# A hand-ordered transformer trunk: attention output splits, output projection and last scan step reordered, seven weight splits moved to GpSimd

## The chip, the cores and the metric

One core of a Trainium2 chip runs the whole kernel. TensorE (PE) multiplies, VectorE (DVE) and ScalarE (ACT) work on its results, GpSimd (POOL) takes small side jobs, and SyncE (SP) issues the DMAs. The metric is the device time of one execution in microseconds. Before the change the median of three runs is 751.57 us (750.9 to 751.59).

## The reference

A trunk of two layers over 256 positions of width 1024: a sparse attention mixer (NSA), a gated MLP, a Mamba-2 mixer (SSD) and a second gated MLP, each between two RMS norms and added to the stream. Cut to what the change touches:

```python
def compress_tokens(t, pos, w1, w2):            # k_cmp and v_cmp, blocks of 32 with stride 16
    ...
    return jax.nn.gelu(flat @ w1) @ w2

def nsa_mixer(h, w_in, cmp_pos, cmp_w1, cmp_w2, w_out):
    proj = h @ w_in
    ...
    kc = compress_tokens(k_cmp, cmp_pos[0], cmp_w1[0], cmp_w2[0])
    vc = compress_tokens(v_cmp, cmp_pos[1], cmp_w1[1], cmp_w2[1])
    ...
    o = (gates[..., 0:1] * o_cmp + gates[..., 1:2] * o_sel + gates[..., 2:3] * o_win).astype(h.dtype)
    return o.reshape(b, s, NSA_Q_DIM) @ w_out

def ssd_scan(x, dt, a, bm, cm):                 # in chunks of 128
    ...
    w = cb[..., None] * lmat * dt_k[:, None]
    y = jnp.einsum("blsgh,bsghp->blghp", w, x_k)
    y = y + jnp.einsum("blgn,bghpn->blghp", c_k, state) * jnp.exp(acs)[..., None]
```

With 256 positions there are four selection blocks and all of them are selected, so the selected branch is a plain causal attention, as the window branch is.

## The kernel before

**Weights.** Every float32 matrix product is made of three rounded ones: a value is split into a high part (a cast on ACT, L56) and a low part (the difference, L57, on DVE or POOL), and high*high, high*low and low*high are added in PSUM. `Weights` (L71) loads a matrix in halves of 128x1024 from HBM into `raw` (512 KB each, L77), and splits each half into `whi` and `wlo`. `raw` has five buffers: the load of a half can be issued only when the half five places before it has been both cast and subtracted. `whi` and `wlo` have five buffers each too, which PE frees.

**Attention (to 160 us).** `ORDER` (L24) is a list of tokens, played by `token` (L458): v values, b the windows of compressed keys (b0) or values (b1), k keys, q queries, h one of four quarters of the compression matrix (h0 and h1 for keys, h2 and h3 for values), m the rest of the compression MLP (m0 keys, m1 values), p scores of a group's head, n softmax scaling, t a transposition of probabilities ("flip"), c and y the output of a group (into PSUM `po`), o the output projection. A `g` or `G` in a token puts the low part of its first or second half on POOL (`lows`, L460). Between bars the tokens are bound to the order of PE. The rest of the order, on every engine, is made by a scheduler from data dependences and the order of the code; within an engine instructions then run strictly in that order.

**The chain of m0** (L299 to L323) goes through all engines: `pc` (PSUM, the products of h0 and h1) is copied to `ph` by ACT, summed by PE (`pht`), copied to `xx` by ACT, worked on by DVE (`t`, L309 to L311), ACT (tanh, L312) and DVE (`hd`, L314, L315), and multiplied by PE (`pkc`, L319). Only then do the keys of compressed blocks exist, which the first scores read.

**Output.** `combine` (L443) adds a token's product to `po`, and with the last one splits `po` into `oT` at once (ACT and DVE). Token o (L489) multiplies two K tiles of `oT` with `nsa_out` into `acc`.

**The scan (460 to 500 us).** `SEQ` (L25) orders the Mamba scan likewise: x transposes a chunk of inputs into PSUM (`px`) and scales it on DVE (L712), m multiplies the masked decays (L732), y is the product of a group (`pys`, L736) and its addition on DVE (L748). `px`, `pys` and `pcb` share two PSUM buffers (tag t).

Of the kernel before, what the change touches and what calls it, by code (L numbers as in the profile page):

```python
# [20 lines left out]
EPS = 1e-6  # L21
T0, T1, N0, N1, SFILL, LAG = 5, 4, 2, 2, 2, 5
FA, FB, FN, CHAIN = 5, 8, 3, 0
ORDER = "v0 b0g k00w q00wG q01 k01 h0g u0 h1 m0 b1 h2 p00 p01 p02 p03 k10g q10 h3 n0 k11 q11 q20w p10 p11 m1 p12 q30w p13 n1 q21 t010 t000 t011w t001w q31 t012 p20 t013w | c0 y010 y011 y012 y013 y000 y001 | p21 t100 p22 t101w p23 t110 n2 t111w t112 p30 t113w | c1 y100 y101 y110 y111 y112 y113 | p31 t210 p32 t211w t200 p33 t212 t201w o00 t213w n3 | c2 y210 y211 y212 y213 y200 y201 | o01 t310 t300 t311w t301w t312 t313w | c3 y300 y301 y310 y311 y312 y313 o10 o11 |"  # L24
SEQ = "X00 X50 X01 X10 X11 X20 X60 X51 X21 X30 X31 X40 X70 X61 f0 X41 X71 Z00 E Z01 a0 Z10 f1 e00 e01 Z11 a1 e02 e03 x00 Z20 e10 e11 Z21 e12 e13 x10 m0 m1 x01 Z30 w0 Z31 y0 f2 w1 a2 e20 e21 e22 e23 x20 x11 Z40 f3 Z41 y1 m2 w2 x21 e30 e31 e32 | e33 a3 x30 | Z50 | m3 y2 x31 Z51 Z60 w3 | y3 | Z61 Z70 | Z71"  # L25
NEG = -1e30

C_ID, C_TRI, C_SUM, C_SEL, C_ONE, C_MS, C_N = 0, 128, 256, 316, 348, 476, 604
# [5 lines left out]
def trunk(ctx, tc, x, gains, consts, masks, params, nsa_in, nsa_vw, cmp_w1, nsa_out,  # L34
# [187 lines left out]
    def nsa(np_, xt, after):  # L222
# [220 lines left out]
        def combine(g, qt, n):  # L443
            po, ph = pos_[g, qt], phs[g, qt, n]
            b, kb = divmod(n, qt + 1)
            end = n == 2 * qt + 1
            for r in range(2):
                mm(po[64 * r:64 * r + 64], vs[:, kb, b, g, :], ph[:, r::2, :], start=False, stop=end)
            if end:
                qs = slice(128 * qt, 128 * qt + 128)  # L450
                split(oT[0][:, 2 * g:2 * g + 2, qs], oT[1][:, 2 * g:2 * g + 2, qs], po)

        oT = [one([128, KT, S], f"ot{n}", F32R) for n in range(2)]
        dummy = one([128, 1], "dummy")
# [3 lines left out]
        def token(z):  # L458
            kind, n, wide = z[0], [int(c) for c in z[1:] if c.isdigit()], "w" in z
            lows = [c for c in range(2) if "gG"[c] in z]  # L460
            if kind == "v":
                values()
            elif kind == "b":
                gs[n[0]] = blocks_of(n[0], wide, lows)
            elif kind == "k":
                keys(*n, wide, lows)
            elif kind == "h":
                kv, u = divmod(n[0], 2)
                if u == 0:
                    pc[kv] = pa([120, 256], "pc")  # L470
                hidden(pc[kv], kv, gs[kv], u, lows)
            elif kind == "u":
                setup()
                nc.sync.dma_start(mc16.rearrange("p a b -> p (a b)"), masks[:, :32])
            elif kind == "m":
                compressed(pc[n[0]], n[0])
            elif kind == "q":
                queries(*n, wide, lows)
            elif kind == "p":
                scores(*n)  # L480
            elif kind == "n":
# [510 lines left out]
```

## Time and profile before

| | before |
|---|---|
| median of 3 runs | 751.57 us |
| the profiled execution | 751.31 us |
| its span, first to last instruction | 749.5 us |
| PE busy | 720.9 us (96%) |
| DVE busy | 573.6 us (77%) |
| ACT busy | 465.5 us (62%) |
| POOL busy | 63.0 us (8%) |
| granted TensorE clock, mean | 0.991 |

PE is busy nearly all the time, so an edit counts where it makes or removes idle time of PE. Busy shares of the other engines are averages: near the end of the span and in the two MLPs they have room, in the attention stage DVE and ACT are at 80 and 68%.

### The profile page before, as it was taken

What the parts mean: (1) busy time and instruction counts of PE and PEld (TensorE: products, weight loads), DVE (VectorE), ACT (ScalarE), POOL (GpSimd) and SP (SyncE); (2) the same over time, 40 slices, a digit from 0 to 9 for tenths busy, and PEclk for the clock granted to TensorE, in tenths of its full rate; (3) what the DMA queues carried; (4) which work ended last, traced back from release to release, by engine and by line L of the source; (5) the groups of instructions that cost most, each with busy time, mean ns of one, the idle gap of its engine ahead of it and who ended that gap; (6) DMA issues with size and microseconds to landing.
All of it is one profiled execution on the core that took longest, in us unless ns stands there. A gap on an engine that the chain in (4) does not pass through costs nothing.

```text
span 749.5 us, 13757 instructions
## 1 busy us (share of the span) xinstructions
PE 720.9 (96%) x5300; PEld 665.4 (89%) x5300; DVE 573.6 (77%) x931; ACT 465.5 (62%) x881; POOL 63.0 (8%) x96
## 2 busy tenths in 40 slices
PE   7998999999999999999999999999989999999996
PEld 5998888679999999997899999898779999999995
DVE  4688998747977767777698878788888967776783
ACT  4576777646665556565785687766556656555651
POOL 2210111211000000000100000024120000000000
PEclk7999999999999999999999999999999999999999
DMA  8864421315656665666355565125645665666531
GB/s 313 276 219 156 161 89 56 112 57 169 218 177 197 195 189 179 188 211 199 118 170 164 189 210 160 67 85 176 215 144 163 204 192 173 199 192 194 176 112 57
DMA packets 35426, 125.95 MB, mean 168 GB/s; under 512 B 4064, under 2 KB 4384, under 8 KB 35360
## 3 DMA queue, kind: packets, MB, share of 16 engines
q1 hardware_dynamic: 35360, 125.07, 51.6%
q8 instruction: 42, 0.69, 0.4%
q14 instruction: 24, 0.20, 0.1%
HBM read 124.00 MB, written 1.05 MB: 167 GB/s over the span
## 4 chain that ended last, share of the span: by engine, by line
PE 74%; DVE 12%; ACT 7%; DMA 3%; issue 2%; POOL 1%; SPq 0%; DVEq 0%; POOLq 0%; ACTq 0%
PE pu L61 43%; PE acc L61 18%; PE pv L61 6%; DVE wlo L57 4%; ACT P L388 2%; PE pt L65 2%; ACT whi L56 1%; DVE P L412 1%; ACT junk L126 1%; PE po L61 1%; DMA gain<-in_gains 1%; PE py L61 1%; DMA raw<-in_ssd_in 1%; DMA raw<-in_ffn_down 1%; DMA raw<-in_ssd_out 1%
## 5 line engine op out<-in xcount | busy, mean ns | idle before, releaser
L57 DVE TENSOR_TENSOR wlo<-raw,whi 128x1024 fp32r<-128x1024 f32 (+1 forms) x220 | 268.1, 1225 | 81.8 <-ACT whi L56 81.2
L56 ACT CAST whi<-raw 128x1024 fp32r<-128x1024 f32 x223 | 231.1, 1044 | 108.6 <-PE pu L61 58.3
L61 PE MATMUL pu<-xhi,whi 128*128 128x256 f32 x1056 | 296.3, 281 | 0.1
L61 PE MATMUL pu<-xhi,wlo 128*128 128x256 f32 x1056 | 295.1, 280 | 0.0
L61 PE MATMUL pu<-xlo,whi 128*128 128x256 f32 x1056 | 294.7, 279 | 0.0
L61 PEld LDWEIGHTS pu<-xhi,whi 128*128 128x128 f32 x1056 | 198.5, 188 | 2.0 <-DVE kd L53 0.3
L61 PEld LDWEIGHTS pu<-xlo,whi 128*128 128x128 f32 x1056 | 198.6, 188 | 1.2
L61 PEld LDWEIGHTS pu<-xhi,wlo 128*128 128x128 f32 x1056 | 198.4, 188 | 0.1
L524 DVE SCALAR_TENSOR_TENSOR cc<-pu,pr,cc 128x255 f32<-128x255 f32 (+2 forms) x248 | 111.3, 478 | 6.4 <-ACT cc L518 3.3
L61 PE MATMUL acc<-whi,hm 128*128 128x512 f32 x352 | 114.6, 390 | 1.0 <-ACT hm L56 1.0
L61 PEld LDWEIGHTS acc<-whi,hm 128*128 128x128 f32 x352 | 66.1, 188 | 14.7 <-ACT hm L56 1.5
L61 PE MATMUL acc<-wlo,hm 128*128 128x512 f32 x176 | 68.9, 392 | 0.0
L518 ACT ACTIVATE cc<-pu,pr 128x256 f32<-128x256 f32 x112 | 57.7, 558 | 8.9 <-PE pu L61 8.8
L56 ACT CAST hm<-cc 128x256 fp32r<-128x256 f32 x44 | 17.8, 405 | 44.9 <-DVE cc L552 44.9
L117 POOL TENSOR_SCALAR ms<-ss 128x1 f32<-128x1 f32 x16 | 7.7, 479 | 420.0 <-ACT junk L126 420.0
L61 PE MATMUL acc<-whi,gw 128*128 128x512 f32 x128 | 41.3, 397 | 0.0
L61 PEld LDWEIGHTS acc<-wlo,hm 128*128 128x128 f32 x176 | 33.0, 188 | 5.6
L61 PE MATMUL pv<-whi,xhi 128*128 128x256 f32 (+1 forms) x128 | 36.8, 300 | 1.0 <-ACT whi L56 0.6
L61 PE MATMUL pv<-whi,xlo 128*128 128x256 f32 (+1 forms) x128 | 35.6, 296 | 1.0 <-DVE xlo L57 0.9
L61 PE MATMUL pv<-wlo,xhi 128*128 128x256 f32 (+1 forms) x128 | 36.0, 293 | 0.0
L57 DVE TENSOR_TENSOR hm<-cc,hm 128x256 fp32r<-128x256 f32 x44 | 18.6, 423 | 14.6 <-ACT hm L56 14.6
L61 PEld LDWEIGHTS acc<-whi,gw 128*128 128x128 f32 x128 | 24.0, 188 | 5.2
(212 smaller groups left out, 885.2 us busy)
## 6 DMA issues: line engine op xcount, KB each, us to landing
raw<-in_ffn_up SPq DMA_DIRECT2D x88, 512.0 KB, 4.4
raw<-in_ffn_down SPq DMA_DIRECT2D x44, 512.0 KB, 4.6
raw<-in_ssd_in SPq DMA_DIRECT2D x40, 512.0 KB, 4.7
raw<-in_nsa_in SPq DMA_DIRECT2D x18, 512.0 KB, 5.2
raw<-in_ssd_out SPq DMA_DIRECT2D x16, 512.0 KB, 4.5
gain<-in_gains SPq DMA_DIRECT2D x8, 512.0 KB, 5.0
raw<-in_cmp_w SPq DMA_DIRECT2D x8, 512.0 KB, 5.2
raw<-in_nsa_out SPq DMA_DIRECT2D x8, 512.0 KB, 4.1
```

The source lines that it names most:

```text
L56: r = copy(hi, src)
L57: eng.tensor_tensor(lo, src, hi.bitcast(F32), op=OP.subtract)
L61: last_mm[0] = nc.tensor.matmul(*a, **k)
L65: last_mm[0] = nc.tensor.transpose(*a)
L117: nc.gpsimd.tensor_scalar(ms, a, b, EPS, op0=OP.mult if isinstance(b, float) else OP.add, op1=OP.add)
L126: nc.scalar.activation(junk, src[c], AF.Square, scale=1.0 / 32, accum_out=ss[:, c:c + 1])
L388: nc.scalar.activation(P[qt][:, hh, b, :], sx[:, b, :], AF.Exp, bias=mx[:, qt, b:b + 1], accum_out=sums[:, qt, hh, b + 1:b + 2])
L412: eng.tensor_scalar(P[qt][:, hh, b, :], P[qt][:, hh, b, :], rr[:, qt, hh, b + 1:b + 2], 1.0, op0=OP.mult, op1=OP.mult)
L518: nc.scalar.activation(c, ps, AF.Identity, bias=pr[:, base + nt:base + nt + 1], scale=pr[:, base + nt - 1:base + nt])
L524: nc.vector.scalar_tensor_tensor(c[:, s:], ps[:, :S - s], wv, c[:, s:], op0=OP.mult, op1=OP.add)
```

## The change

1. The tokens h0g, h1, h2, h3 become h0gG, h1gG, h2gG, h3gG: the low parts of all eight halves of the compression matrix are made on POOL, where one of the eight was before.
2. `combine` no longer splits `po`. A new function `heads_out` and a token s do it; s0 and s1 stand behind the next group's first scores, s2 and s3 among the flips and outputs.
3. Token o takes one K tile instead of two (o00 becomes o000 and o001), and these are spread among the flips of the last two groups.
4. In SEQ, `y2 x31` becomes `x31 y2`.

```diff
-ORDER = "v0 b0g k00w q00wG q01 k01 h0g u0 h1 m0 b1 h2 p00 p01 p02 p03 k10g q10 h3 n0 k11 q11 q20w p10 p11 m1 p12 q30w p13 n1 q21 t010 t000 t011w t001w q31 t012 p20 t013w | c0 y010 y011 y012 y013 y000 y001 | p21 t100 p22 t101w p23 t110 n2 t111w t112 p30 t113w | c1 y100 y101 y110 y111 y112 y113 | p31 t210 p32 t211w t200 p33 t212 t201w o00 t213w n3 | c2 y210 y211 y212 y213 y200 y201 | o01 t310 t300 t311w t301w t312 t313w | c3 y300 y301 y310 y311 y312 y313 o10 o11 |"
+ORDER = "v0 b0g k00w q00wG q01 k01 h0gG u0 h1gG m0 b1 h2gG p00 p01 p02 p03 k10g q10 h3gG n0 k11 q11 q20w p10 p11 m1 p12 q30w p13 n1 q21 t010 t000 t011w t001w q31 t012 p20 t013w | c0 y010 y011 y012 y013 y000 y001 | p21 s0 t100 p22 t101w p23 t110 n2 t111w t112 p30 t113w | c1 y100 y101 y110 y111 y112 y113 | p31 s1 t210 p32 t211w t200 p33 t212 t201w o000 t213w n3 | o001 c2 y210 y211 y212 y213 y200 y201 o010 s2 t310 t300 o011 t311w t301w o100 t312 t313w o101 c3 y310 y311 y312 y313 y300 y301 s3 o110 o111 |"
@@ -446,9 +446,11 @@
             end = n == 2 * qt + 1
             for r in range(2):
                 mm(po[64 * r:64 * r + 64], vs[:, kb, b, g, :], ph[:, r::2, :], start=False, stop=end)
-            if end:
+
+        def heads_out(g):
+            for qt in (1, 0):
                 qs = slice(128 * qt, 128 * qt + 128)
-                split(oT[0][:, 2 * g:2 * g + 2, qs], oT[1][:, 2 * g:2 * g + 2, qs], po)
+                split(oT[0][:, 2 * g:2 * g + 2, qs], oT[1][:, 2 * g:2 * g + 2, qs], pos_[g, qt])
 
         oT = [one([128, KT, S], f"ot{n}", F32R) for n in range(2)]
         dummy = one([128, 1], "dummy")
@@ -486,13 +488,15 @@
                 compressed_out(*n)
             elif kind == "y":
                 combine(*n)
+            elif kind == "s":
+                heads_out(*n)
             else:
-                u, i = n
+                u, i, k = n
                 if not accs:
                     accs.extend([ps_([128, 512], "acc") for c in range(2)] for i in range(2))
                 if u not in wos:
                     wos[u] = weights(nsa_out[u], 2, D, lows=lows)
-                out_mm(accs[i], i, [(oT, 2 * u + k, wos[u], k) for k in range(2)], u == 0, False)
+                out_mm(accs[i], i, [(oT, 2 * u + k, wos[u], k)], u + k == 0, False)
 
         accs = []
         rigid = False
```

The scheduler's order follows from this. On POOL, in the attention stage (wlo_548 is the low part of the second half of h0, wlo_576 and wlo_582 those of h1, wlo_694 and wlo_700 of h2, wlo_899 and wlo_905 of h3; wlo_813 belongs to keys and was there before):

```order
 L57 TENSOR_TENSOR wlo_451<-raw_448,whi_450 128x1024
 L57 TENSOR_TENSOR wlo_542<-raw_539,whi_541 128x1024
+L57 TENSOR_TENSOR wlo_548<-raw_545,whi_547 128x1024
+L57 TENSOR_TENSOR wlo_576<-raw_573,whi_575 128x1024
+L57 TENSOR_TENSOR wlo_582<-raw_579,whi_581 128x1024
+L57 TENSOR_TENSOR wlo_694<-raw_691,whi_693 128x1024
+L57 TENSOR_TENSOR wlo_700<-raw_697,whi_699 128x1024
 L57 TENSOR_TENSOR wlo_813<-raw_810,whi_812 128x1024
+L57 TENSOR_TENSOR wlo_899<-raw_896,whi_898 128x1024
+L57 TENSOR_TENSOR wlo_905<-raw_902,whi_904 128x1024
```

Seven subtractions have come from DVE, six of them in one row with wlo_542 and wlo_813 around them.

On ACT, around the chain of m0, before (ph_601, xx_606 and t1_608 are m0's; whi_699 is the second half of h2, whi_812 and whi_818 the halves of the next keys):

```order
L301 COPY ph_601<-pc_538 120x256
L56 CAST whi_699<-raw_697 128x1024
L307 COPY xx_606<-pht_603 128x120
L56 CAST whi_812<-raw_810 128x1024
L312 ACTIVATE t1_608<-t1_608 128x120
L56 CAST whi_818<-raw_816 128x1024
L322 CAST kd0_136<-pkc_616 128x4x15
```

and after the change:

```order
L56 CAST whi_699<-raw_697 128x1024
L301 COPY ph_601<-pc_538 120x256
L56 CAST whi_812<-raw_810 128x1024
L307 COPY xx_606<-pht_603 128x120
L312 ACTIVATE t1_608<-t1_608 128x120
L322 CAST kd0_136<-pkc_616 128x4x15
L56 CAST whi_818<-raw_816 128x1024
```

The casts of raw_697 and raw_810 have moved ahead of the copies ph and xx, so that each copy now stands behind a load.

On PE, the flips of the last group, before (pt are the flips, acc the output projection):

```order
L61 MATMUL acc_1687<-whi_1696,ot1_208 128x512
L65 MATMUL pt_1781<-ident_74,cs1_200 128x128
L65 MATMUL pt_1785<-ident_74,P1_1522 128x128 x4
L65 MATMUL pt_1792<-ident_74,cs1_200 128x128
L65 MATMUL pt_1796<-ident_74,P0_1521 128x128 x4
L65 MATMUL pt_1803<-ident_74,P1_1522 128x128 x4
L65 MATMUL pt_1810<-ident_74,P0_1521 128x128 x4
L65 MATMUL pt_1817<-ident_74,P1_1522 128x128 x4
L65 MATMUL pt_1824<-ident_74,P1_1522 128x128 x4
```

and after:

```order
L65 MATMUL pt_1786<-ident_74,cs1_200 128x128
L65 MATMUL pt_1790<-ident_74,P0_1521 128x128 x4
L61 MATMUL acc_1686<-whi_1696,ot0_207 128x512
L61 MATMUL acc_1686<-wlo_1697,ot0_207 128x512
L61 MATMUL acc_1686<-whi_1696,ot1_208 128x512
L61 MATMUL acc_1687<-whi_1696,ot0_207 128x512
L61 MATMUL acc_1687<-wlo_1697,ot0_207 128x512
L61 MATMUL acc_1687<-whi_1696,ot1_208 128x512
L65 MATMUL pt_1803<-ident_74,P1_1522 128x128 x4
L65 MATMUL pt_1810<-ident_74,P0_1521 128x128 x4
```

The eight flips stood in one row; now six matmuls of the projection stand behind each pair.

## Rows read from the trace of the kernel before

**Rows 1.** Busy time by stretch, 40 to 160 us, the sum (PE, PEld, DVE, ACT, POOL):
```profile
sum 120.00, PE 111.53 PEld 98.76 DVE 96.87 ACT 82.17 POOL 17.76; mean PE 9.29 PEld 8.23 DVE 8.07 ACT 6.85 POOL 1.48
```
**Rows 2.** Waits of PE from 40 to 165 us: total us, times, longest.
```profile
PE pkc L61 <- DVE hd L315: 2.1, 1, 2.1
PE sb L61 <- ACT P L388: 1.6, 3, 0.8
PE sa L61 <- ACT P L388: 1.6, 3, 1.3
...
PE pt L65 <- ACT ct L424: 0.8, 1, 0.8
...
PE pt L65 <- ACT pht L435: 0.4, 2, 0.2
```
**Rows 3.** The chain that ended last, 42 to 64 us: start, us, what.
```profile
46.97 1.82 DVE wlo L57 x2
...
54.68 2.33 DVE t L310
...
57.04 0.30 DVE t L311
...
58.29 0.66 PE pkc L61 x4
```
**Rows 4.** Timeline of POOL, 25 to 60 us: start, us, what [idle before <- releaser].
```profile
54.55 2.38 POOL L57 TENSOR_TENSOR wlo<-raw,whi 128x1024 fp32r<-128x1024 f32 x1 [15.35 <-ACT whi L56]
```
**Rows 5.** Timeline of DVE, the same operation of m0 and of m1.
```profile
54.60 2.41 DVE L310 TENSOR_SCALAR t<-t 128x120 f32<-128x120 f32 x1
...
89.52 0.21 DVE L310 TENSOR_SCALAR t<-t 128x120 f32<-128x120 f32 x1
```
**Rows 6.** Timeline of ACT, 42 to 55 us, casts of weight halves.
```profile
42.78 2.00 ACT L56 CAST whi<-raw 128x1024 fp32r<-128x1024 f32 x2
...
45.30 2.01 ACT L56 CAST whi<-raw 128x1024 fp32r<-128x1024 f32 x2
...
53.42 1.06 ACT L56 CAST whi<-raw 128x1024 fp32r<-128x1024 f32 x1 [0.43 <-DMA raw<-in_nsa_in]
```
**Rows 7.** Timeline of the DMA queue (SP), 48 to 50 us.
```profile
48.22 1.46 SPq L77 DMA_DIRECT2D raw<-in_nsa_in  x2
```
**Rows 8.** The page, part 6: DMA issues, count, KB each, median us to landing.
```profile
raw<-in_nsa_out SPq DMA_DIRECT2D x8, 512.0 KB, 4.1
```
**Rows 9.** Timeline of POOL, 502 to 506 us.
```profile
502.62 1.29 POOL L792 TENSOR_TENSOR sq<-sq 128x512 f32<-128x512 f32 x1 [13.16 <-ACT sq L791]
503.99 1.61 POOL L793 TENSOR_TENSOR sq<-sq 128x256 f32<-128x256 f32 x1
```
**Rows 10.** Timeline of DVE, the same stretch.
```profile
503.46 1.54 DVE L57 TENSOR_TENSOR wlo<-raw,whi 128x1024 fp32r<-128x1024 f32 x1 [1.17 <-ACT whi L56]
```
**Rows 11.** Timeline of PE, 72 to 80 us, the quarter h3 of the compression.
```profile
76.48 0.38 PE L61 MATMUL pc<-whi,gs 128*120 128x256 f32 x1 [0.41 <-ACT whi L56]
...
77.74 0.38 PE L61 MATMUL pc<-wlo,gs 128*120 128x256 f32 x1
```
**Rows 12.** Timeline of DVE, the masked decays of the last scan step.
```profile
484.10 2.36 DVE L732 SCALAR_TENSOR_TENSOR E<-E,cb 128x1024 f32<-128x1024 f32 x2
```
**Rows 13.** Timeline of PE, the transposes of the last scan input.
```profile
487.39 0.63 PE L65 MATMUL pt<-ident,xs 128*128 128x128 f32 x4 [1.58 <-DVE xs L748]
```
**Rows 14.** The chain that ended last, the projection behind them, a later `pys`.
```profile
488.02 5.61 PE pu L61 x48
...
494.98 1.90 PE py L61 x32
```
**Rows 15.** Timeline of PE, the first transposes.
```profile
9.88 1.54 PE L65 MATMUL pt<-ident,xn 128*128 128x128 f32 x6 [3.34 <-DVE xn L146]
```
**Rows 16.** Busy time by stretch after them (PE, PEld, DVE, ACT, POOL, PEclk, DMA, GB/s).
```profile
10.00:16.00 6.00, 5.43 (x24) 4.90 (x25) 4.92 (x7) 4.70 (x9) 0.86 (x2) 0.50 1.02 411
16.00:20.00 4.00, 4.00 (x23) 4.00 (x23) 3.78 (x5) 1.91 (x4) 0.00 (x0) 0.60 1.01 386
```

More of the change, by code (lines that the diff above doesn't have):

```diff
@@ L23 @@
 FA, FB, FN, CHAIN = 5, 8, 3, 0
-ORDER = "v0 b0g k00w q00wG q01 k01 h0g u0 h1 m0 b1 h2 p00 p01 p02 p03 k10g q10 h3 n0 k11 q11 q20w p10 p11 m1 p12 q30w p13 n1 q21 t010 t000 t011w t001w q31 t012 p20 t013w | c0 y010 y011 y012 y013 y000 y001 | p21 t100 p22 t101w p23 t110 n2 t111w t112 p30 t113w | c1 y100 y101 y110 y111 y112 y113 | p31 t210 p32 t211w t200 p33 t212 t201w o00 t213w n3 | c2 y210 y211 y212 y213 y200 y201 | o01 t310 t300 t311w t301w t312 t313w | c3 y300 y301 y310 y311 y312 y313 o10 o11 |"
-SEQ = "X00 X50 X01 X10 X11 X20 X60 X51 X21 X30 X31 X40 X70 X61 f0 X41 X71 Z00 E Z01 a0 Z10 f1 e00 e01 Z11 a1 e02 e03 x00 Z20 e10 e11 Z21 e12 e13 x10 m0 m1 x01 Z30 w0 Z31 y0 f2 w1 a2 e20 e21 e22 e23 x20 x11 Z40 f3 Z41 y1 m2 w2 x21 e30 e31 e32 | e33 a3 x30 | Z50 | m3 y2 x31 Z51 Z60 w3 | y3 | Z61 Z70 | Z71"
+ORDER = "v0 b0g k00w q00wG q01 k01 h0gG u0 h1gG m0 b1 h2gG p00 p01 p02 p03 k10g q10 h3gG n0 k11 q11 q20w p10 p11 m1 p12 q30w p13 n1 q21 t010 t000 t011w t001w q31 t012 p20 t013w | c0 y010 y011 y012 y013 y000 y001 | p21 s0 t100 p22 t101w p23 t110 n2 t111w t112 p30 t113w | c1 y100 y101 y110 y111 y112 y113 | p31 s1 t210 p32 t211w t200 p33 t212 t201w o000 t213w n3 | o001 c2 y210 y211 y212 y213 y200 y201 o010 s2 t310 t300 o011 t311w t301w o100 t312 t313w o101 c3 y310 y311 y312 y313 y300 y301 s3 o110 o111 |"
+SEQ = "X00 X50 X01 X10 X11 X20 X60 X51 X21 X30 X31 X40 X70 X61 f0 X41 X71 Z00 E Z01 a0 Z10 f1 e00 e01 Z11 a1 e02 e03 x00 Z20 e10 e11 Z21 e12 e13 x10 m0 m1 x01 Z30 w0 Z31 y0 f2 w1 a2 e20 e21 e22 e23 x20 x11 Z40 f3 Z41 y1 m2 w2 x21 e30 e31 e32 | e33 a3 x30 | Z50 | m3 x31 y2 Z51 Z60 w3 | y3 | Z61 Z70 | Z71"
 NEG = -1e30
```

## The prediction

> **What bounds the kernel now.** I read the page first: PE is busy nearly all the span, so the question is where it idles. The sum of the stretches from 40 to 160 us shows 111.53 us of PE in 120 [rows 1]: about 8.5 us idle at most to be won in the attention stage, where nearly all of the change lies. Then the waits of PE [rows 2] say what ends the idle time: once 2.1 us for `hd` (the compression chain m0), 3.2 us in six places for the exponentials that free score buffers, and 1.2 us for the flips' copies. Then the chain of waits from 42 to 64 us [rows 3] shows why `hd` is late: the path runs through DVE's weight splits and through one operation, L310, of 2.33 us, before it comes to PE's `pkc` at 58.29. All times that follow are in the clock of this execution.
>
> **Seven splits on POOL, the key chain.** Removed from DVE: seven subtractions of about 1.1 us (the one at 503.46 took 1.54, of which it stood 0.45 behind a POOL operation that ended at 503.91) [rows 9, 10], some 8 us of 96.87 that DVE works there [rows 1]. Added to POOL: seven of 2.38 us [rows 4], twice as long. POOL has the time; what counts is who waits.
>
> Three things hang on the end of a split: PE's products of that half, the buffer `raw` of that half, and DVE, since the two engines block each other. For the last, L310 took 2.41 us beside a POOL split that ran from 54.55 to 56.93, and 0.21 us in the second chain with no POOL work beside it [rows 4, 5]: it waited until POOL had ended. And it goes both ways: POOL's L793 took 1.61 us when DVE's split was waiting before it [rows 9, 10]. I read this as taking turns.
>
> So, step by step. The cast of h0's second half ends at 43.8 (first of two from 42.78, 1.0 each) [rows 6]. POOL: h0's second half to 46.2, h1's first to 48.6. DVE's split for b1 is waiting by then (its cast ended at 47.31 [rows 6], and only one scaling of queries more stands before it), so it takes the next turn, to 49.7; h1's second half then runs to 52.1. Before, DVE had done it by 48.2 (the splits from 46.97) [rows 3]. PE comes to it at about 49.6 and idles 2.5 us; the products end at 53.1.
>
> The `raw` buffer of h1's second half is the one that the first half of the next keys needs. That load was issued at 48.22, right behind the split [rows 7], and its cast waited for the landing until 53.42, so 5.2 us [rows 6]. Now the issue is at 52.1, the landing at 57.3, the cast done at 58.4. On ACT the copy `xx` of m0 used to stand ahead of this cast and now stands behind it: it ends at about 58.6. With the cast done POOL starts that half's split at 58.4 (the two of h2 are over by 58.0) and holds DVE until 60.8; L309 and L310 come in the middle, as L310 did before. From L311 to `pkc` it takes 58.29 - 57.04 = 1.25 us [rows 3], with 0.2 for L310: `pkc` at 62.3 in place of 58.29, 4.0 later. Five more matmuls stand behind `pkc` than before, at 5.61/48 = 0.117 us [rows 14]: 0.6. The scores start **4.6 us late**.
>
> Bounds: with POOL keeping the port (h1 done at 51.0), the landing in 4.1 us as the loads of the output weights did [rows 8], and no blocked L310, `pkc` comes at 58.2 and the loss is 0.5 us; if both L309 and L310 are blocked by different POOL splits, 2.4 more than my value, 7.0. I take 4.6, because the collision with the split of the same keys is in the trace of before [rows 4, 5] and both orders of ACT put that cast next to `xx`.
>
> The Trainium skill speaks against the move: "SBUF — State Buffer", section "Who interferes with whom", has one port pair shared by the two engines as a lock that the first holds for its whole instruction while the other fully blocks, for a two-port mode of DVE and for a DVE instruction with two SBUF inputs. L310 agrees (2.41 us beside 0.21). By that rule DVE's split for b1, with two SBUF inputs, takes its turn as I count it; by the row alone only operations like L310 are blocked, h1 would be done 1.1 us earlier and the sum be that much smaller.
>
> **The last quarter, h3.** PE waited for the cast of its second half until 76.48 and found the low part ready at 77.74 [rows 11]. On POOL the low part is 2.38 us behind the cast: 78.85. PE now asks for it after eight matmuls, at 77.4, but its arrival is what the next products wait for: 78.85 - 77.74 = **1.1 us late**. The first half's low part costs less than the 0.41 that it waited for that cast anyhow [rows 11], so nothing. Bounds 0 (PE, 4.6 late, finds other work) and 2.4 (DVE takes a turn first).
>
> **Output splits behind the next scores.** Nothing is added or removed: the same casts and subtractions, later. ACT's exponentials come earlier by the 0.4 to 0.8 us of those casts, but only for the group after the first does ACT's order change. The waits for exponentials are 3.2 us [rows 2]; with DVE lighter by two splits after 62 us I take a quarter, **-0.8**, between 0.5 lost (DVE's remaining splits bunch in front of the maxima) and all 3.2 won.
>
> **Output projection among the flips.** The flips waited 0.8 and 0.4 us for copies of the ones before [rows 2]. Six matmuls now stand behind each pair of flips, over 1 us of PE work, which covers these waits. The projection's own inputs are long split, and its last part still stands behind the last outputs, as before. **-1.2**, between 0 and -1.4.
>
> **Scan.** PE waited 1.58 us at 487.39 for L748 to free a buffer [rows 13]. Now the transposes come first, but L712, which empties their buffer, stands behind both L732 on DVE (484.10 to 486.46 [rows 12]), so it ends at 487.1; the second half of the product `pys` needs that buffer, takes 0.95 (half of 1.90), and the projection follows at 488.1, where it was at 488.02 [rows 14]. The wait changes its name: **0**, within 0.8 lost (POOL's addition comes later beside DVE) and 1.6 won.
>
> **The sum.** 4.6 + 1.1 - 0.8 - 1.2 + 0 = 3.7 us on the profiled execution's 751.31, of which 749.5 are span: 755.0. That execution is 0.26 under the median, which I leave inside the range: **755.0 us**, slower by 0.5%. By its own bounds the likeliest case lies at 753.2 to 757.5.
>
> **The rivals.**
> *A. DVE was the bound and is freed: faster.* The chain before `pkc` is DVE's splits and L310 [rows 3]. If five fewer splits let m0 run early, the loss is the 0.5 of the lower bound, h3 costs nothing, and -1.8 of the 3.2, -1.4 at the flips are kept: -2.7, 748.6. It decides for this if `xx` ends before 56.5 and POOL isn't in the middle of a split then. Against it: five buffers of `raw`, and the row of L310.
> *B. The loss is absorbed: no change.* The head costs about 2.5 (landing in 4.1 us and one blocked operation only), half of the 3.2 is won back since PE is late and ACT has caught up: 2.5 + 0.5 - 1.6 - 1.2 = 0.2, 751.5. For it: six waits that can shrink. Against it: the exponentials wait for PE's scores, and shift with them.
> *C. The clock falls too: slower still.* PE idled 3.34 us before 9.88, and the granted clock then stood at 0.50 (the 1.2 GHz level) from 10 to 16 and averaged 0.60 to 20, at least 9 us at the low level [rows 15, 16]. In my count PE idles about 3.9 us before `pkc`. If that is enough, PE runs at half speed until about 70: half of some 8 us of work lost, 4.0, less 0.5 of waits that it hides: 758.5. For it: the idle time is longer than that one. Against it: it is split by short work, and the 2.1 us of before left the clock at 1.00.
>
> **Chances.** A 0.20, B 0.15, forecast 0.45, C 0.20. A measurement of this kernel can tell about 0.2%, 1.5 us. Slower: the forecast and C, 0.65; same 0.15; faster 0.20. The range from 749.4 to 758.8 leaves half of A below, and the upper part of C above.
>
> **What would show it.** Right: POOL with splits back to back from 43.8 to about 58, `pc` waiting over 1.5 us for a low part, `pkc` waiting for `hd` by 3 us or more, L309 or L310 over 2 us, waits for `ct` and `pht` gone, and a wait of over 1 us inside `pys` in the scan. Wrong: `pkc` before 60, the loads after h1 issued as early as before, or a gain in the flips beyond 1.4 us. A clock row below 1.00 between 58 and 75 us says C.

## The result, and the profile after

The changed kernel takes 759.84 us (median of 4, 758.79 to 761.59), the kernel before 751.24 us beside it: ratio 1.0121 [1.0106, 1.0136], 8.6 us slower where 3.7 were forecast. The profiled execution took 759.34 us; its span is 757.0, which is 7.5 more than before.

Where the 7.5 us lie is seen when the attention stage is cut at four events that both traces have: the first product of h0 (`pc`), the first score (`sb`), the first product into `pvc` (the end of m1), and the first transposition of the next stage. Busy time by stretch (length, then PE, PEld, DVE, ACT, POOL, granted clock, DMA share, GB/s), before:

```profile
46.17:60.01 13.84, 10.80 (x91) 10.40 (x89) 12.79 (x17) 9.17 (x16) 2.38 (x1) 1.00 0.88 293
60.01:92.68 32.67, 30.86 (x254) 29.78 (x252) 29.39 (x70) 25.30 (x74) 3.53 (x8) 1.00 0.43 138
92.68:167.70 75.02, 70.95 (x498) 58.33 (x498) 54.69 (x127) 47.51 (x147) 13.58 (x28) 1.00 0.25 83
```

and after:

```profile
46.02:64.50 18.48, 13.37 (x90) 12.74 (x89) 10.87 (x12) 9.41 (x16) 13.74 (x6) 0.86 0.65 229
64.50:101.28 36.78, 32.41 (x252) 30.78 (x251) 32.13 (x70) 26.79 (x76) 11.32 (x10) 0.98 0.45 146
101.28:175.18 73.90, 70.26 (x498) 58.30 (x498) 52.44 (x125) 45.97 (x145) 15.41 (x28) 1.00 0.23 71
```

I call the stretches I, II and III. I is 4.64 us longer, II 4.11 longer, III 1.12 shorter: 7.63, which is the whole difference. PE's busy time in I is longer only because its clock was lower (0.86 of 18.48 us: 2.6 us lost). In II 2.6 us are more waiting, and 1.5 us a longer busy time of PE for the same matmuls: group by group the counts are those of before. The clock is the smaller part of these 1.5, since in w_after (below), with 1.00 in II, PE is still busy for 32.02 us there; what makes the rest is not shown. III is shorter by 0.7 of busy time, again for the same matmuls, and by 0.4 of waits.

The waits of PE from 40 to 165 us, after (total us, times, longest), which answer to [rows 2]:

```profile
PE pc L61 <- POOL wlo L57: 4.0, 4, 2.1
PE pkc L61 <- DVE hd L315: 2.7, 1, 2.7
PE pvc L61 <- DVE hd L315: 1.4, 1, 1.4
PE pt L65 <- ACT ct L424: 1.2, 2, 0.8
PE sb L61 <- ACT P L388: 1.0, 1, 1.0
PE sb L61 <- DVE A L361: 0.6, 2, 0.5
PE sa L61 <- ACT P L388: 0.5, 2, 0.4
```

Two waits are new, `pc` for POOL's low parts and `pvc` for the end of m1; the exponentials' waits have halved (3.2 to 1.5), those for `ct` have grown. PE also waits 0.6 us for `A`, the scaled queries.

The head, step by step. POOL (answers to [rows 4]):

```profile
43.73 16.03 POOL L57 TENSOR_TENSOR wlo<-raw,whi 128x1024 fp32r<-128x1024 f32 x6 [4.70 <-ACT whi L56]
76.29 2.38 POOL L57 TENSOR_TENSOR wlo<-raw,whi 128x1024 fp32r<-128x1024 f32 x1 [16.53 <-ACT whi L56]
82.08 2.37 POOL L57 TENSOR_TENSOR wlo<-raw,whi 128x1024 fp32r<-128x1024 f32 x1 [3.41 <-ACT whi L56]
```

DVE beside it (answers to [rows 5]):

```profile
47.75 1.82 DVE L57 TENSOR_TENSOR wlo<-raw,whi 128x1024 fp32r<-128x1024 f32 x1 [0.24 <-ACT whi L56]
...
49.94 2.92 DVE L57 TENSOR_TENSOR wlo<-raw,whi 128x1024 fp32r<-128x1024 f32 x1
...
57.40 2.51 DVE L309 TENSOR_TENSOR t<-xx 128x120 f32<-128x120 f32 x1 [4.08 <-ACT xx L307]
59.94 0.22 DVE L310 TENSOR_SCALAR t<-t 128x120 f32<-128x120 f32 x1
```

Of the seven moved splits five stand in this row, and the sixth of the row is the keys' split, which was on POOL before; h3's two follow by themselves. The six have no gap, 16.03 us for what alone takes 6 times 2.38, or 14.3; the rest is DVE's turns. DVE's own two splits of b1 took 1.82 and 2.92 instead of some 1.2, and L309 stood until the keys' split ended at 59.76.

ACT and the DMA queue (answer to [rows 6, 7]):

```profile
56.16 1.05 ACT L56 CAST whi<-raw 128x1024 fp32r<-128x1024 f32 x1 [2.33 <-DMA raw<-in_nsa_in]
57.12 0.25 ACT L307 COPY xx<-pht 128x120 f32<-128x120 f32 x1
```

```profile
46.17 2.67 SPq L77 DMA_DIRECT2D raw<-in_cmp_w  x2
51.80 3.65 SPq L77 DMA_DIRECT2D raw<-in_nsa_in  x4
57.46 2.66 SPq L77 DMA_DIRECT2D raw<-in_cmp_w  x2
```

The keys' load goes out at 51.80 (48.22 before), and `xx` stands behind its cast. So `pkc` comes 15.43 us behind the first `pc` instead of 12.12.

Behind the first scores, PE waits for both low parts of h3 and at `pvc` (answers to [rows 11], where the low part was ready):

```profile
78.73 0.38 PE L61 MATMUL pc<-wlo,gs 128*120 128x256 f32 x1 [0.49 <-POOL wlo L57]
```

```profile
84.50 0.38 PE L61 MATMUL pc<-wlo,gs 128*120 128x256 f32 x1 [1.06 <-POOL wlo L57]
```

```profile
101.28 0.51 PE L61 MATMUL pvc<-pr,hd 128*15 128x64 f32 x6 [1.43 <-DVE hd L315]
```

The granted clock, stretch by stretch, around the two long waits:

```profile
50.00:52.00 2.00, 0.17 (x1) 0.17 (x2) 2.00 (x2) 1.78 (x3) 2.00 (x2) 1.00 0.55 207
52.00:54.00 2.00, 2.00 (x13) 2.00 (x14) 1.28 (x2) 1.42 (x2) 2.00 (x1) 0.65 0.52 131
54.00:56.00 2.00, 2.00 (x12) 2.00 (x11) 0.00 (x0) 0.00 (x0) 2.00 (x2) 0.50 0.91 320
56.00:62.00 6.00, 3.32 (x28) 3.12 (x28) 3.52 (x5) 1.51 (x3) 3.76 (x2) 1.00 0.87 329
62.00:64.00 2.00, 2.00 (x14) 2.00 (x14) 0.66 (x2) 1.26 (x2) 0.00 (x0) 0.71 0.44 147
64.00:66.00 2.00, 2.00 (x11) 2.00 (x10) 1.99 (x3) 1.05 (x1) 0.00 (x0) 0.50 0.07 18
```

It fell to 0.50 (the 1.2 GHz level) twice, from 52.6 to 56.0 and from 62.8 to 66.2, each time while PE was busy again after idling 2.1 and 2.7 us. Before, it stayed at 1.00 here.

The scan: the wait at the transposes [rows 13] is gone and stands inside `pys` instead, where L716 comes behind both L736 (L712 and L732 of the kernel before; answers to [rows 12]):

```profile
494.36 1.09 PE L61 MATMUL py<-E,xd 128*64 128x128 f32 x16 [1.74 <-DVE xd L716]
```

```profile
491.34 2.36 DVE L736 SCALAR_TENSOR_TENSOR E<-E,cb 128x1024 f32<-128x1024 f32 x2
493.62 0.68 DVE L716 TENSOR_TENSOR xd<-pt,dt 128x512 f32<-128x512 f32 x1
```

From the next stage's first transposition to the end it is 581.8 us in both.

### The profile page after: what moved, and what is told of

Read it like the earlier page. It is cut to its first block, busy times and chain, and to the rows that moved or that the text cites. A ratio compares the mean times of both kernels' runs of the same rounds, so it can differ in the third digit from the quotient of the medians.

```text
span 757.0 us, 13760 instructions
## 1 busy us (share of the span) xinstructions
PE 723.8 (96%) x5300; PEld 668.2 (88%) x5300; DVE 570.7 (75%) x924; ACT 465.3 (61%) x881; POOL 87.2 (12%) x103
## 4 chain that ended last, share of the span: by engine, by line
PE 70%; DVE 8%; ACT 5%; issue 3%; DMA 2%; POOL 1%; DVEq 0%; POOLq 0%; ACTq 0%
PE pu L61 41%; PE acc L61 18%; PE pv L61 4%; DVE wlo L57 3%; PE pt L65 2%; ACT whi L56 1%; ACT P L388 1%; PE po L61 1%; ACT junk L126 1%; PE py L61 1%; DVE P L412 1%; DMA raw<-in_ssd_in 1%; DMA raw<-in_ffn_down 1%; DMA raw<-in_ssd_out 1%; DVE gw L793 1%
## 5 line engine op out<-in xcount | busy, mean ns | idle before, releaser
L57 DVE TENSOR_TENSOR wlo<-raw,whi 128x1024 fp32r<-128x1024 f32 (+1 forms) x213 | 263.6, 1243 | 77.8 <-ACT whi L56 77.3
L61 PE MATMUL pv<-whi,xhi 128*128 128x256 f32 (+1 forms) x128 | 36.8, 300 | 1.0 <-ACT whi L56 0.6
L57 POOL TENSOR_TENSOR wlo<-raw,whi 128x1024 fp32r<-128x1024 f32 x11 | 28.0, 2562 | 40.4 <-ACT whi L56 40.4
L57 DVE TENSOR_TENSOR hm<-cc,hm 128x256 fp32r<-128x256 f32 x44 | 18.6, 423 | 14.6 <-ACT hm L56 14.6
```

Source lines behind the costliest of these rows:

```text
L57: eng.tensor_tensor(lo, src, hi.bitcast(F32), op=OP.subtract)
L61: last_mm[0] = nc.tensor.matmul(*a, **k)
```

## The experiments

Ratios are to the kernel before, run on the same chip.

**The two halves of the change.** Everything but the seven subtractions, and the subtractions alone:

```diff
 e1_no_pool (from the changed kernel)        e2_pool_only (from the kernel before)
-h0gG u0 h1gG m0 b1 h2gG ... h3gG            -h0g u0 h1 m0 b1 h2 ... h3
+h0g u0 h1 m0 b1 h2 ... h3                   +h0gG u0 h1gG m0 b1 h2gG ... h3gG
```

> The changed kernel with the four tokens h0g, h1, h2, h3 as before, so that DVE makes the seven low parts again; output splits, projection by single K tiles and the scan's swap stay. Theory (all of the loss is the seven subtractions on GpSimd): 750.3 to 751.2 us, 0 to 0.9 us under the kernel before (the traces show 0.5 us won at the flips and 0.16 lost in the scan); the wait of pkc is 2.1 us again and the granted clock stays at 1.00 from 50 to 70 us. Rival (the later output splits or the projection cost something themselves, hidden in the trace of after by the later scores): 752.5 or more.

> The kernel before with nothing but h0gG, h1gG, h2gG, h3gG: the seven subtractions alone. Theory (they are the whole loss): 8 to 9.5 us over the kernel before, some 760 us, with PE waiting some 2 us for a low part near 52 us and some 2.7 us for hd near 61 us, and the granted clock at 0.5 in two stretches of some 3.4 us. Rival (the other edits give part of the loss, or only the sum of both makes the waits long enough): 4 to 6 us over the kernel before.

e1: 749.99 us, 0.9982 [0.9971, 0.9992], faster by 1.35 us; I 13.38, II 32.69, III 73.68, with the clock at 1.00 in all three. Its III:

```profile
92.22:165.90 73.68, 70.22 (x499) 58.34 (x498) 54.73 (x127) 47.59 (x147) 14.50 (x28) 1.00 0.26 85
```

PE's busy time in III is that of the changed kernel (70.26), with II as before. So the 0.7 us of shorter busy time come from the other edits and not from a move of work between the stretches. e2: 760.68 us, 1.0127 [1.0111, 1.0142], with both waits and both falls. The seven subtractions are the whole loss; the other three edits gain a little, most of it (1.34 us in the profiles) in III.

**Is that gain the scan's?** e1 with `y2 x31` as before:

```diff
-m3 x31 y2 Z51
+m3 y2 x31 Z51
```

> The kernel before with the later output splits and the projection by single K tiles only: the scan's order and all of GpSimd's work as before. Theory (the scan's swap only renames a wait; what e1_no_pool gains, 1.35 us, is all in the attention stage): the time of e1_no_pool within 0.5 us, some 749.7. Rival 1 (in e1_no_pool's profile the granted clock fell for 3.4 us in the scan, and the swap causes that): 1 to 1.7 us under e1_no_pool. Rival 2 (the gain is the swap's): the time of the kernel before.

750.07 us, 0.9985 [0.9975, 0.9994]: the time of e1, so the swap gains nothing. The profiles show more than the times. From the second group of `py` products to the next stage's first `acc` it is 30.4 us without the swap (before, e2, e8) and 30.8 to 30.9 with it (the changed kernel twice, e10): the swap loses about 0.5 us, too little for the times. In e1's profile, where the clock is at 0.50 from 486.9 to 490.3, the same stretch takes 32.39 us; that execution took 750.89 us, 0.9 over its median. And in e8's profile the clock is at 0.50 from 58.2 to 61.6, behind PE's wait of 1.81 us at `pkc`: with the head's order as in e1 its I takes 14.40 us instead of 13.38, and II gives nothing back (32.72, 32.69).

**Which subtractions?** Keys only, values only, and h3 alone and alone left out:

```diff
 e5_h01  (from before)      -h0g u0 h1       +h0gG u0 h1gG
 e6_h23  (from before)      -h2 ... h3       +h2gG ... h3gG
 e17_h3  (from before)      -h3              +h3gG
 e18_no_h3 (from after)     -h3gG            +h3
```

> The kernel before with h0gG and h1gG only: three of the seven subtractions on GpSimd, those of the keys' compression; h2 and h3 stay on DVE. Theory (the head of the loss is these three: PE's wait for h1's second half, the load behind it, xx and L309 or L310 held by GpSimd; the rest of the loss is h2 and h3): PE waits about 2 us for h1's second low part, pkc comes 2.5 to 3.5 us later than in the kernel before, no wait of over 1 us for h3's low parts or for pvc, and 4 to 6 us over the kernel before with whatever clock falls follow. Rival 1 (it takes the whole row of six on GpSimd to hold the loads; three hold nothing): at most 1.5 us over the kernel before. Rival 2 (these three are all of the loss): 8 us or more.

> The kernel before with h2gG and h3gG only: the four subtractions of the values' compression on GpSimd. Theory: pkc as in the kernel before within 1 us, PE waits about 0.5 and 1.0 us for the low parts of h3 and some 1.4 us at pvc, 2 to 3.5 us over the kernel before, no fall of the clock near 50 to 66 us. Rival 1 (h2's splits on GpSimd alone hold the loads and pkc): pkc 2 us or more later, 5 us or more over the kernel before. Rival 2 (the waits for h3 and pvc come only from the late head): at most 1 us over the kernel before.

> The kernel before with h3gG only: the last two of the seven subtractions on GpSimd. Theory (the part of the loss behind the first scores, some 3 us, is these two: PE waits for both low parts, and the values' chain m1 ends in a wait at pvc): first scores as in the kernel before within 0.5 us, PE waits of some 0.5 to 0.8, 1.0 and 1.4 us at the two low parts and at pvc, no fall of the clock before pvc, and 2.5 to 4 us over the kernel before. Rival (these waits need the late head; on time, they are taken from waits that were there already): at most 1 us over the kernel before.

> The changed kernel with h3 for h3gG: its last two low parts on VectorE again, the others on GpSimd. Theory: the first scores as late as in the changed kernel, no wait at pvc or for h3's low parts, 2.5 to 4 us under the changed kernel, some 5 over the kernel before. Rival (the late head alone sets the loss, h3's waits replace others): within 1 us of the changed kernel.

| | us | ratio | I | II | III |
|---|---|---|---|---|---|
| before | | | 13.84 | 32.67 | 75.02 |
| e5 (h0, h1) | 754.62 | 1.0042 [1.0029, 1.0054] | 17.67 | 33.42 | 75.11 |
| e6 (h2, h3) | 758.25 | 1.0104 [1.0087, 1.0120] | 18.57 | 36.81 | 74.79 |
| e17 (h3) | 755.27 | 1.0050 [1.0030, 1.0070] | 13.60 | 37.18 | 76.13 |
| e18 (all but h3) | 755.02 | 1.0046 [1.0032, 1.0059] | 17.50 | 33.39 | 73.64 |
| after (all) | 759.84 | 1.0121 [1.0106, 1.0136] | 18.48 | 36.78 | 73.90 |

II is 36.8 to 37.2 us where h3 is on POOL and 33.4 or less where it isn't, however late the head is. I is 17.5 to 18.6 with h0 and h1 on POOL (e5, e18), but also with h2 and without them (e6), and 13.6 with h3 alone. So h3's part adds to the head's, and within the head either half is enough: my theory for e6 (`pkc` on time, no fall of the clock, 2 to 3.5 us) was wrong. e5 lost less than the 4 to 6 us that I expected, and e18 gained more than 2.5 to 4. In e6 `xx` is early, and each step of m0 on DVE waits for the end of one split of POOL's row:

```profile
52.02 1.01 DVE L309 TENSOR_TENSOR t<-xx 128x120 f32<-128x120 f32 x1 [0.93 <-ACT xx L307]
53.07 2.27 DVE L310 TENSOR_SCALAR t<-t 128x120 f32<-128x120 f32 x1
55.37 2.32 DVE L311 TENSOR_TENSOR t<-t,xx 128x120 f32<-128x120 f32 x1
```

This makes `pkc` 1.4 us late against the first `pc` (13.50 us behind it, 12.12 before). The other 3.3 us of e6's head lie behind `pkc`: 19 of b1's products stand there instead of 10, PE having waited 4.56 us for `hd`, and they run at the low clock (0.50 from 57.8 to 64.6).

PE's waits of e17 (whose first scores are on time) have three of the changed kernel's in II:

```profile
PE pvc L61 <- DVE hd L315: 1.4, 1, 1.4
...
PE pc L61 <- POOL wlo L57: 1.2, 2, 0.9
...
PE sb L61 <- DVE A L361: 0.8, 2, 0.5
```

That e17 would have no fall of the clock ahead of `pvc` was wrong: it stands at 0.50 from 58.2 to 61.6, behind a wait of 1.65 us at `pkc`, and again from 95.8 to 99.1.

Why `pvc` is late: h3's second half holds its `raw` buffer until POOL is through, so the loads of the output weights go out at 84.47 (the changed kernel) instead of 77.71 (before); 4.6 of that is the late head, and in e17, whose head is on time, they go out 2.3 us later against the first `pc` (33.86 us behind it, 31.54 before). In DVE's order two of their splits stand between m1's steps (the changed kernel; before, one split of 1.22 stood there and L309 ran at 88.89, L311 at 91.43):

```profile
96.13 0.28 DVE L309 TENSOR_TENSOR t<-xx 128x120 f32<-128x120 f32 x1
96.33 1.22 DVE L57 TENSOR_TENSOR wlo<-raw,whi 128x1024 fp32r<-128x1024 f32 x1
...
97.89 0.21 DVE L310 TENSOR_SCALAR t<-t 128x120 f32<-128x120 f32 x1
98.02 1.22 DVE L57 TENSOR_TENSOR wlo<-raw,whi 128x1024 fp32r<-128x1024 f32 x1
...
99.76 0.27 DVE L311 TENSOR_TENSOR t<-t,xx 128x120 f32<-128x120 f32 x1
```

This is read from the order and not tried by itself, and it is not all: against the first score m1 falls behind step by step, `pht` by 0.8 us, `xx` by 1.8, L309 by 2.8, L311 by 3.8 and `pvc` by 4.1, so that only some 1.1 of it lie between L309 and L311.

**Which step of the head?** The keys' split or h1's second half back on DVE:

```diff
 e3_k10_dve (from after)     -k10g     +k10
 e12_h1g    (from after)     -h1gG     +h1g
```

> The changed kernel with k10 for k10g: the low part of the first half of the next keys, which was on GpSimd in the kernel before too, is made on DVE, so that GpSimd's row ends with h2. PE's order puts pkc 9 matmuls later. Theory (L309 took 2.51 us because GpSimd was in that split): L309 and L310 below 0.4 us each, hd some 1 to 2.3 us earlier (DVE has one split of 1.1 us more to make there), PE's wait for hd under 1 us, no second fall of the clock, and 2.5 to 4 us under the changed kernel (4.6 to 6.1 over the kernel before). Rival 1 (the late load and cast ahead of xx set hd, and DVE is held by h2's last split instead): pkc not before 60.5, at most 1 us under the changed kernel. Rival 2 (L309 is slow for itself): L309 over 2 us again.

> The changed kernel with h1g for h1gG: the low part of h1's second half is made on DVE again, all the others stay on GpSimd; PE and ACT keep their order. Theory (PE's first wait and the late load of the next keys come from this split's place in GpSimd's row of six, the rest of pkc's lateness from the keys' own split, which then starts when h2's are over, 2.4 us earlier): the wait of 2.09 us falls under 0.8, the load is issued 1 to 2 us earlier, L309 or L310 is still held by GpSimd for over 1 us, pkc comes 1 to 2 us earlier, and the time is 1 to 2.5 us under the changed kernel (6 to 7.5 over the kernel before). Rival 1 (DVE's split is itself held by GpSimd's row until the row ends): the wait stays near 2 us or grows, no gain. Rival 2 (this one split causes nearly all of the loss at the head): 4 us or more under the changed kernel.

e3: 756.10 us, 1.0069 [1.0051, 1.0087]. L309 and L310 take 0.27 and 0.22, `pkc` comes 14.23 us behind the first `pc` (15.43 in the changed kernel), PE waits 0.55 for it, and the second fall is gone. So POOL's split is what makes L309 slow. e12: 760.76 us, 1.0123 [1.0107, 1.0140], no gain. PE's wait did shrink to 0.7 and the load went out at 50.10 instead of 51.80, but it landed at 56.51 (56.08 in the changed kernel), 6.4 us after its issue instead of 4.3, and L309 took 2.37 us beside POOL again. So `pkc` came 15.24 us behind the first `pc`, with a wait of 3.79 us for `hd`, and the clock stood at 0.50 from 60.5 to 67.3, so that the first score came 1.0 us later than in the changed kernel. Freeing the buffer earlier bought nothing; what held that load is not shown.

**What does the clock cost?** The falls looked like 3.4 us of PE's time (half of 6.8). The first attempt filled PE's waits with matmuls of zeros (the edits are cut to their main lines):

```diff
+            fill(8)     # e4 only: in the wait for h1's second low part
+            fill(18)    # behind pht (10 in e4a)
```

> The changed kernel and 26 further bf16 matmuls of 512 columns of zeros into a PSUM tile that nobody reads: 8 where PE waits for the second low part of h1, 18 behind pht, where PE waits for hd. No other wait is changed. Theory (the clock fell because of these two waits; the first fall lies beside the wait for hd and costs nothing, the second stretches the scores): granted clock 1.00 from 50 to 70 us, L309 still over 2 us, pkc still at about 61.4, and the time 1.5 to 2 us under the changed kernel (some 7 over the kernel before). Rival 1 (each fall costs its own 1.7 us): 3 to 3.5 us under the changed kernel, 5.2 over the kernel before. Rival 2 (the clock falls for another reason): it falls again and the time is that of the changed kernel, 8.6 over the kernel before, or some us more.

> The changed kernel and 10 of the same matmuls, behind pht only, so that the wait for h1's second low part stays empty. Theory: the first fall of the granted clock (near 53 us) is there, the second (near 63) is not, and the time is that of the kernel with both fills within 0.4 us, 1.5 to 2 us under the changed kernel. Rival 1 (each fall costs 1.7 us): 1.7 us over the kernel with both fills. Rival 2 (the wait before pkc has nothing to do with the second fall): both falls as in the changed kernel, 8.6 us over the kernel before.

764.84 us, 1.0192 [1.0168, 1.0217], and 762.21 us, 1.0149 [1.0135, 1.0163]. Neither is a test: with the extra matmuls the scheduler moved `pkc` ahead of 19 of b1's products in e4a and of 22 in e4, and in e4 the copy `ph` behind a cast as well, so that PE ran the zeros in place of work, waited all the same (2.52 for `hd` in e4a, 3.40 for `ph` in e4), and did the work afterwards. With `pkc` issued from its place among b1's products the other engines keep their order (on PE `pht` stands seven products earlier in e14):

```diff
+hook.extend([33, later.pop()])     # pkc is issued behind b1's 33rd product
+fill(10)                           # directly ahead of pkc (e13); 4 + 18 in e14
```

> The changed kernel with 10 bf16 matmuls of 512 columns of zeros (into a PSUM tile that nobody reads) directly ahead of pkc, where PE waits 2.68 us for hd; pkc and its copies are issued from the place in b1 where PE's order has them anyway, so that, apart from the 10, the order of every engine is that of the changed kernel. Theory (that wait made the granted clock fall near 63 us, and the fall stretches scores that the rest waits for): pkc as late as in the changed kernel, its wait 0.4 to 0.8 us, one fall only (near 52 us), and 1.4 to 2 us under the changed kernel, some 6.9 over the kernel before. Rival 1 (the fall is hidden by later waits): one fall only, but the time of the changed kernel within 0.4 us, 8.6 over the kernel before. Rival 2 (the wait has nothing to do with the clock): two falls, 8.6 over the kernel before.

> The same with 4 more matmuls of zeros in PE's wait of 2.09 us for h1's second low part, and 18 instead of 10 ahead of pkc; the order of the other engines is that of the changed kernel, on PE only pht comes two matmuls or so earlier. Theory (the first fall lies beside the wait for hd, whose end is set by a load, a cast and GpSimd, so it costs nothing): no fall between 50 and 70 us, pkc as late as in the changed kernel within 0.5 us, and the time of the kernel with the 10 alone within 0.5 us. Rival (each fall costs its own 1.7 us): 1.7 us under that kernel, 5.2 over the kernel before.

e13: 760.96 us, 1.0116 [1.0095, 1.0138]; e14: 758.76 us, 1.0104 [1.0085, 1.0123]. The stretches I, II and III of e14's profile:

```profile
45.25:63.08 17.83, 15.76 (x110) 12.61 (x111) 10.08 (x12) 9.45 (x16) 13.81 (x6) 1.00 0.69 237
63.08:100.57 37.49, 32.14 (x254) 30.08 (x252) 33.17 (x70) 26.83 (x76) 11.33 (x10) 0.99 0.44 143
100.57:177.39 76.82, 73.14 (x497) 61.12 (x498) 52.43 (x125) 46.04 (x145) 15.45 (x28) 0.96 0.21 68
```

The clock is 1.00 in I now, and I and II together are 55.32 us, against 55.26 with both falls. I gains 0.65, II gives it back as waits (one of 0.5 us at `pc` for DVE is new). e13, with the first fall in its place, has 55.01 (17.50 and 37.51). Executions of the changed order without fills lie between 55.0 and 55.6, so up to `pvc` these two falls cost nothing that shows. Not every fall ahead of `pvc` is free: e8, with one, takes 1.0 us more in I and II together than e1, and e12, with one of 6.8 us (but another place for h1's split), 1.0 more than the changed kernel.

In e13 and e14 the clock also fell at the wait for `pvc`, in e14 for 6.8 us from 100.2, and III grew by 2.9, nearly all of the 3.4 that these lose (e13: 76.81). Theory and rivals were all half right: the falls ahead are free, as said of the first, and no fall came where the waits were filled. Whether the fills brought the one at `pvc` is not shown, for one comes there without them too (w_after, below).

To meet the clock at other moments without touching any order, the start got 24 matmuls of zeros instead of 14, in time in which PE waits [rows 15]:

```diff
-    for n in range(14):
+    for n in range(24):
```

> The kernel before with 24 instead of 14 matmuls of zeros at the start, in time in which PE waits 3.34 us for the first inputs; nothing else moves on any engine. It is the ground for the next run and measures what the low clock of the first 20 us costs. Theory: the clock stays at 1.00 from 9 us on, and since the stretch from 10 to 20 us also waits for loads (the DMA engines are busy all of it), the gain is 1 to 3 us, not the 5.1 that half of 10.24 us would be. Rival: the loads set the end of that stretch alone: within 0.5 us of the kernel before.

> The changed kernel with the same 24 matmuls at the start. The attention stage then meets the granted clock's steps at other moments. Theory (two falls in the attention stage cost about 1 to 2 us of the 8.6, since the first lies beside the wait for hd and later waits take up part of the second): 7 to 9 us over the kernel before plus what w_before gives (its time less that of the kernel before); in the stretch from pc's first matmul to the next stage's first transposition (121.5 us in the kernel before, 129.2 in the changed one) 127 to 130 us, whatever the falls. Rival (the falls cost their full 3.4 us): a run of this kernel with no fall in that stretch needs 125.8 us there.

> The changed kernel itself once more, for a second profile of it and for the mean granted clock of each timed run: does the clock fall at the same two places in every execution, and how far does the time follow it? Theory (waits take up most of what the falls stretch): from the run with the highest mean clock to the one with the lowest the time grows by less than half of the clock cycles lost. Rival (falls cost in full): by as much as the cycles lost, that is 0.76 us for each 0.001 of the mean clock.

w_before: 750.15 us, 0.9988 [0.9977, 1.0000]: 0.9 us, just under the 1 to 3 expected, and in its profile the clock still stood at 0.50 from 11.1 to 18.0 us (in those of w_after and e16 it did not). w_after: 759.84 us, 1.0118 [1.0105, 1.0131], 9.7 us over w_before where 7 to 9 were expected. In its profile the clock falls at the same two waits, and a third time at 100.9, behind `pvc`; II and III:

```profile
63.02:99.77 36.75, 32.02 (x253) 30.15 (x252) 32.21 (x69) 26.79 (x76) 11.30 (x10) 1.00 0.44 147
99.77:175.20 75.43, 71.78 (x498) 59.82 (x498) 52.42 (x125) 45.97 (x145) 15.42 (x28) 0.98 0.21 69
```

III is 1.5 us longer than with 1.00, for 1.7 us of cycles lost. The stretch from `pc` to the next stage took 131.06 us, over the 127 to 130 that I expected for any falls, since the third was not in that count. The changed kernel again: 759.85 us, 1.0117 [1.0104, 1.0130], the two falls at the same two waits, I 18.24, II 36.77, III 73.86. Its four runs lie between 758.75 us at a mean clock of 0.990 and 760.66 at 0.987, too few and too rounded for a slope. So in this order the falls in I and II cost little, and one behind `pvc` costs 1.5 us and comes in some executions.

What brings a fall is not settled. Both come in all four profiles with the seven splits on POOL and no fill (the changed kernel twice, e2, w_after). e5 and e18 have the same order of PE up to the first score and wait 2.55 and 2.31 us at `pkc`, but only the first fall. With the head's order of before, the clock falls behind `pkc`'s wait in e8 (1.81) and e17 (1.65) and not in the kernel before (2.14), w_before (1.67) and e1 (1.63). So the falls stand behind waits of PE, but the waits alone do not tell whether one comes, and a profile each of e3, e13 and e14 does not prove that the shorter waits are what kept the clock up.

**A version that beats both.** The other edits kept, and the last low part taken off POOL, which before made too [rows 4]; then also the start with 24:

```diff
 e10_k10 (from e1_no_pool)   -k10g            +k10
 e16     (from e10_k10)      -range(14)       +range(24)
```

> The kernel with no added subtraction on GpSimd (as e1_no_pool) and k10 for k10g as well: GpSimd makes no low part between 45 us and the outputs. Theory (before and in e1_no_pool L310 loses over 2 us because GpSimd is in the split of the same keys): L309 and L310 below 0.4 us each, pkc 0.5 to 2 us earlier against the first product of h0 than in e1_no_pool (DVE puts splits of 1.1 us between the steps of the chain in exchange), and 748.0 to 749.7 us, 0.3 to 2 us under e1_no_pool. Rival (the two or three splits that DVE now makes inside the chain cost what L310 gives): the time of e1_no_pool within 0.5 us, or more.

> The fastest kernel so far (e10_k10: later output splits, projection by single K tiles, the scan's swap, no low part on GpSimd after 45 us) with the 24 matmuls at the start. Theory: the two gains are in different stretches and add up: 1 to 3 us under e10_k10, 745.5 to 748. Rival: as in w_before's rival, the time of e10_k10 within 0.5 us.

e10: 748.85 us, 0.9962 [0.9947, 0.9977]; e16: 746.88 us, 0.9953 [0.9936, 0.9969]. In e10 the same operations as in [rows 5]:

```profile
52.37 0.28 DVE L309 TENSOR_TENSOR t<-xx 128x120 f32<-128x120 f32 x1
52.57 1.22 DVE L57 TENSOR_TENSOR wlo<-raw,whi 128x1024 fp32r<-128x1024 f32 x1
53.71 0.22 DVE L310 TENSOR_SCALAR t<-t 128x120 f32<-128x120 f32 x1
```

`pkc` is 1 us later than in the kernel before against the first `pc` (13.12) and 1.5 later than in e1, where I expected it earlier, since DVE puts whole splits between the steps; but PE has 2.2 us more of other work ahead of the first score (13.02 us in I instead of 10.80) and no wait of over 0.25 us at `pkc`, so I and II together are 45.70 us instead of 46.51. Both beat the kernel before. The intervals of e1 and e10 overlap a little, and e16's gain on e10 is inside the intervals; e16's profile has no fall of the clock before the end, e10's has one from 89.2 to 92.6.

## Why the prediction was right and wrong

*The key chain, 4.6: right in its steps, in size by luck.* The first scores are 4.64 us late. POOL and DVE took turns: DVE's first split of b1 ran when h1's first half was done, then POOL (h1's second half over at 51.8, 52.1 forecast), then DVE again. The load went out at 51.80 (52.1), its cast ended at 57.2 (58.4), `xx` at 57.4 (58.6), the keys' split held L309 to 59.8 (60.8). The landing in 4.3 us instead of 5.2 made `pkc` 3.3 late instead of 4.0, and the second fall of the clock, which the sum did not have, filled it up again by some 0.8. The Trainium skill, "SBUF — State Buffer", section "Who interferes with whom", has the other engine fully blocked for a whole instruction of the first, where DVE runs in a two-port mode or reads two inputs from SBUF. The traces agree for two inputs (L311, 2.32 us in e6) and for L310 with one (2.27), whose mode no trace shows.

*h3, 1.1: the step that failed.* The term counts one late low part, and stretch II lost 4.1 us. I counted the second low part alone (1.06 measured) and let the first cost nothing (0.49). Above all I followed the `raw` buffer behind h1 but not behind h3, and no further than PE's products: the next loads went out 2.3 us later still than the head made them (e17), and m1, a second chain like m0, fell behind at each step and ended in a wait of 1.43 us at `pvc`. e17 and e18 show that h3's two splits make this alone, late head or not: 3.8 us when only they are added (ratio 1.0050), and 4.6 us of the stage gone when only they are taken out (124.53 us for I to III instead of 129.16). How much of it comes by the late loads is not shown.

*Output splits and flips, -2.0: too much.* With the scan's swap, which gains nothing, they gave 1.35 (e1). The exponentials' waits, a quarter of which I counted as won, are 3.2 us in e1 too; they are 1.5 only in the kernels with h3 on POOL, where PE waits elsewhere instead. The wait of 0.76 us for `ct`, two thirds of the flips' term, stayed in every kernel: no projection matmuls stand between the flip that waits and the one whose copy it waits for. About half of the gain in III is a shorter busy time of PE for the same matmuls, which I had not counted; why is not shown. In the changed kernel III gained 1.12.

*The scan, 0: right.* The wait went from 1.58 at the transposes to 1.74 in `pys`. The stretch is 0.5 us longer by it, inside the bound of 0.8, and the time did not change (e8).

*The rivals.* "DVE freed" and "absorbed" fell: DVE was lighter, but the chain is bound by what waits for POOL. Half of the exponentials' waits did go, as "absorbed" had it, but new waits took their place. "The clock falls too" happened, and twice, and its 758.5 us lies nearest to the result; yet that is not why. Ahead of `pvc` the falls took time that PE would have waited (e13, e14).

The sum as measured: I 4.6, II 4.1, III -1.1, scan 0, so 7.6 against 4.6 + 1.1 - 2.0. The medians are 8.6 apart and the two profiled executions 8.0, of which 0.5 lie outside their spans. What makes the other 0.6 is not shown; a fall behind `pvc` in some executions, as w_after's profile has one, would do it.

## What to carry to other kernels

Where a pipeline's buffers are freed by an engine, moving work to a slower one delays every load that waits for those buffers; follow each of them to the chain that it ends in, not only the first. Small steps of a critical chain on VectorE should have no long GpSimd work on SBUF beside them: each one can wait out a whole instruction. A fall of the clock, like any lost time of PE, counts only where PE is the bound: look for a wait behind it before it is added to the sum. A forecast that comes out right can hide two errors: here one fall made up for a load that landed early.

## What the hardware showed

- An operation of VectorE of 0.2 to 0.3 us took 2.3 to 2.5 us beside a GpSimd subtraction of 2.38 us, and three in a row each waited for the end of one (e6). GpSimd's own took 3.3 us when VectorE had its turn first.
- The granted clock fell at or right behind PE's waits of 2.1 and 2.4 to 2.7 us in each of the four profiles with all seven splits on POOL and no fill (the changed kernel twice, e2, w_after). It also fell behind 1.81 us (e8) and 1.65 (e17), and stayed at 1.00 behind 2.55 (e5), 2.31 (e18) and 2.14 (the kernel before).
- What a fall costs depends on what stands behind it: nothing that shows in I and II of the changed kernel, 1.0 us of 1.7 lost in e8, 1.5 of 1.7 in w_after's III, 2.9 of 3.4 in e14's.
- A load that was issued 1.7 us earlier landed no earlier (e12); the cause is open.
